# HGRN2 levels: one fill of two PSUM banks, joint factor tiles, both pairs' projections first, a general PSUM ring of two

## The chip, the cores and the metric

The kernel runs on one core of a Trainium2 chip. The metric is the device time of one execution in microseconds. A core has TensorE (PE, with the weight loads shown apart as PEld), VectorE (DVE), ScalarE (ACT), GpSimd (POOL) and SyncE (SP, which issues DMAs here). Each engine executes its own instructions in order; engines wait for each other by semaphores.

## The reference, cut to what matters

The program is one step of a two-layer backbone on 128 prompt and 256 sample tokens (384 together, width 1024). Layer 0 has two mixers behind one input projection: windowed attention with 8 heads of 64 (A), and a bidirectional HGRN2 with 4 heads of 128 (B), a gated linear recurrence:

```python
qa, ka, va, qb, ib, ff, fb, gb = split(h @ w_in)
f = lb + (1 - lb) * sigmoid(z);   k = 1 - f            # a gate for each direction
# one direction, over time t (qc = q * dk**-0.5, cum = cumsum(log f))
attn[t, s] = sum_k qc[t, k] * exp(cum[t, k] - cum[s, k]) * k[s, k]     # s <= t
o = attn @ v  +  (qc * exp(cum)) @ s_start             # within a chunk + from the state
s_end = exp(last) * s_start + (k * exp(last - cum))^T @ v
ob = rms_norm(o_fwd + o_bwd, gnorm) * silu(gb)
y = concat([oa, ob]) @ w_out
```

Then come a residual with layer norm, a gated feed-forward network, and layer 1 with two other attention mixers, which the change leaves alone. All is in fp32.

## The kernel before, in words

Every large product is made of three fp32r matmuls (lines 127 to 129): the weights are split into a high part wh (ACT, line 122) and a low part wl (DVE, line 123) as they arrive, the activations into hH and hL. Weights go through rings of three tiles.

The kernel is written in a framework with a scheduler: it sets each engine's order beforehand, from the order in which the program is written, shifted by an offset for each part of it (the table AHEAD; a larger number comes earlier), and from which operands it expects to be ready. Tiles come from pools; a tile whose slots are all in use must wait until one is read out.

PSUM in layer 0 is opened as three slots "ps" of one bank (attention's scores s, transposed probabilities pt, values ov, and in hg_out tk, up, ho, ty), three "pj" for projections and output accumulators o, one "lv" for the levels, and one more for the adaLN vectors of later stages (ada_acc, line 203; such a step is four matmuls).

mixer_ab (line 818) computes layer 0's mixers. HGRN2's four heads go as two pairs. For a pair, proj_fm makes q and two gates, with features on partitions (2 heads x 384 tokens in a row of 768). hg_levels (line 861) then builds the matrix attn for each of six blocks of 128 tokens (2 heads x 3). It does that by doubling: a diagonal step, then seven levels with spans of 1, 2, 4 to 64 tokens. The factors Fq and Fk (forward), Bq and Bk (backward) hold q and k times the gates' products up to the span's border. In a level ACT copies halves of the four factors into a mixed key tile Kc and query tile Qc (lines 890 to 893), PE multiplies six blocks (line 872, tile hs), DVE merges the part of the result that belongs to the level into the matrix AT with a mask (copy_predicated, line 911), and DVE multiplies the factors by the next gates' products (line 900), and those among themselves (nB, lines 907 and 908). The six blocks need two fills of the one "lv" bank, four blocks and two.

hg_out (line 921) follows for a pair: keys transposed (tk, 933), the states' update (up, 938), the output (ho, 950 to 954), its sum of squares (ACT, 958), an inverse root on POOL (line 110), scaling and gate on DVE (963, 968), a transposition (ty, 971), and the split into hH and hL (132, 133).

attention (line 725) runs through pairs of tiles: two scores s (722, with the mask at 1116) for a query tile, row maximum (640), bias nm (608), exponential (643), transposes pt (673), their evacuation by ACT or DVE (656, 658), ov (679), and the put of the result as hH and hL (663, 664). out_first starts the output projection on what is there (tiles o). The boundary then completes it; its dense stretch begins where no more of hg_out is awaited.

The order of the program at the end of mixer_ab is: a_ctx, the projections of keys and values and of queries, the levels of pair 0, the projections of pair 1, those of the values ib and the gate gb, the levels of pair 1, attention, hg_out 0, out_first, hg_out 1.

Of the kernel before, what the change touches and what calls it, by code (L numbers as in the profile page):

```python
# [20 lines left out]
P = 128  # L21
D = 1024
KD = 8
NTOK = 384
# [5 lines left out]
AHEAD = {"w": 1500, "w0": -700, "lv0": -30, "lv1": 0, "attA": 400, "attC": 400, "attD": 100, "fin": 500, "qs": -1500,  # L30
# [11 lines left out]
def tile_backbone_step(ctx, tc, I, O):  # L42
# [10 lines left out]
    psum = {}  # L53
# [7 lines left out]
    def lvt(name):  # L61
        return psum["lv"].tile([P, 512], F32, tag="lv", name=name)
# [755 lines left out]
    def mixer_ab():  # L818
# [4 lines left out]
        M = Slots(es, {"one": (1, 0), "pr": (4, 768), "pt": (6, 512), "qS": (2, 1536), "qf": (3, 768),  # L823
                       "X": (8, 768), "at": (2, 768), "vB": (2, 768), "kq": (3, 768), "t2": (5, 512),
# [4 lines left out]
        def hg_tiles():  # L829
            return M.tile("qf", F32), [M.tile("X", F32) for _ in range(4)], [M.tile("qf", F32) for _ in range(2)]  # L830
# [9 lines left out]
        def ev_f(pr, d, X, f):  # L840
            def ev(j, acc):
                c = slice(4 * d + 2 * pr + j, 4 * d + 2 * pr + j + 1)
                sl = slice(j * NTOK, (j + 1) * NTOK)
                sg = M.sm.tile([P, NTOK], F32, tag="sg", name="sg")
                nc.scalar.activation(sg, acc, AF.Sigmoid)
                nc.vector.tensor_scalar(out=X[2 + d][:, sl], in0=sg, scalar1=C["nomlb"][:, c],
                                        scalar2=C["omlb"][:, c], op0=ALU.mult, op1=ALU.add)
                nc.vector.tensor_scalar(out=f[d][:, sl], in0=sg, scalar1=C["omlb"][:, c], scalar2=C["lb"][:, c],
                                        op0=ALU.mult, op1=ALU.add)
                nc.vector.tensor_scalar(out=f[d][:, sl], in0=f[d][:, sl], scalar1=1e-30, scalar2=None, op0=ALU.max)  # L850
            return ev

        def hg_proj(pr):
            q, X, f = hg_tiles()
            proj_fm(w, 768 + 256 * pr, ev_q(q))
            proj_fm(w, 1792 + 256 * pr, ev_f(pr, 0, X, f))
            proj_fm(w, 2304 + 256 * pr, ev_f(pr, 1, X, f))
            return q, X, f


        def hg_levels(q, X, f, out):
            Fq, Bq, Fk, Bk = X
            nc.vector.tensor_tensor(out=Fq, in0=q, in1=f[0], op=ALU.mult)
            nc.vector.tensor_tensor(out=Bq, in0=q, in1=f[1], op=ALU.mult)
            AT = M.tile("at", F32).rearrange("p (b t) -> p b t", b=6)

            def scores(Kc, Qc, take):
                for b0, nb in ((0, 4), (4, 2)):
                    pp = lvt("hs").rearrange("p (b t) -> p b t", b=4)
                    for b in range(nb):  # L870
                        bs = slice((b0 + b) * P, (b0 + b + 1) * P)
# [3 lines left out]
            def diag(pp, bl, nb):  # L875
                nc.vector.tensor_tensor(out=AT[:, bl, :], in0=pp, in1=ident.unsqueeze(1).to_broadcast([P, nb, P]),
                                        op=ALU.mult)

            Kc = M.tile("kq", F32)
            nc.vector.tensor_tensor(out=Kc, in0=Fk, in1=Bk, op=ALU.add)  # L880
            scores(Kc, q, diag)
            yield
            Bf, Bb = f
            for lv in range(7):
                m = 1 << lv
                G = 2 * NTOK // (2 * m)
                V = lambda a: a.rearrange("p (g h m) -> p g h m", h=2, m=m)
                Kc = M.tile("kq", F32)
                Qc = M.tile("kq", F32)
# [5 lines left out]
                bf = Bf.rearrange("p (g h w) -> p g h w", h=2, w=w_)[:, :, :, 0]  # L895
                bb = Bb.rearrange("p (g h w) -> p g h w", h=2, w=w_)[:, :, :, 0]
                bc = lambda a: a.unsqueeze(2).to_broadcast([P, G, m])
                for eng, T, hh, fac in ((nc.vector, Fk, 0, bf[:, :, 1]), (nc.vector, Bk, 1, bb[:, :, 0]),
                                        (nc.vector, Fq, 1, bf[:, :, 0]), (nc.vector, Bq, 0, bb[:, :, 1])):
                    eng.tensor_tensor(out=V(T)[:, :, hh, :], in0=V(T)[:, :, hh, :], in1=bc(fac), op=ALU.mult)  # L900
                if lv == 0:
                    nB = M.sm.tile([P, 2, NTOK], F32, tag="nB", bufs=1, name="nB")
                    Bf, Bb = nB[:, 0, :], nB[:, 1, :]
                    nf, nb_ = Bf, Bb
                else:
                    nf, nb_ = bf[:, :, 0], bb[:, :, 0]
# [3 lines left out]
                def merge(pp, bl, nb):  # L910
                    nc.vector.copy_predicated(AT[:, bl, :],
                                              C["lmask"][:, lv, :].unsqueeze(1).to_broadcast([P, nb, P]), pp)
# [4 lines left out]
            for d, B in enumerate((Bf, Bb)):  # L917
                nc.vector.tensor_copy(out=eb[:, d, :], in_=B.rearrange("p (g w) -> p g w", w=64)[:, :, 0])
            out.extend((AT, eb))

        def hg_out(pr, X, AT, eb, vB):
            Fq, Bq, Fk, Bk = X
# [85 lines left out]
        st0 = hg_tiles()  # L1008
# [71 lines left out]
        ps1 = open_psum(3, 3, 1)  # L1080
# [70 lines left out]
        with ahead("lv1"):  # L1151
            drain(hg_levels(*st1, lv1))
# [301 lines left out]
    for l in range(2):  # L1454
# [6 lines left out]
        with tc.tile_pool(name="bnd", bufs=1) as b1:  # L1461
# [3 lines left out]
                     x_in if l == 0 else x_mid, False, first, lvt if l == 0 else None, part)  # L1465
# [63 lines left out]
```

## Time and profile before

| | us |
|---|---|
| three runs | 1095.95, 1096.12, 1098.69; median 1096.12 |
| the profiled execution | 1095.94 |
| its span, first instruction to last | 1094.1 |
| input projections of layer 0 | 58.7 to 188.3 |
| attention, levels, hg_out 0 | 188.3 to 235.0 |
| levels 2 to 6 of pair 1, hg_out 1 | 235.0 to 272.1 |
| dense output projection of layer 0 | from 272.1 |

Times inside the execution count from the start of the span. A busy share is the part of a stretch in which an engine executes; a wait is the idle time before an instruction, with the engine and instruction that ended it. The granted clock is a share of TensorE's full speed. A line of the timeline groups records of one operation that follow each other ("x4" is four of them); a matmul of fp32 operands of 128x128 is two records, a transposition one. PE's matmuls are pipelined, so that one that takes 0.39 us can be followed by another after 0.22.

### The profile page before, as it was taken

Reading aid. Unit: us, or ns where it says so; the run is one execution under the profiler, and the core shown is the slowest. Engines: PE = TensorE matmul, PEld = TensorE weight load, DVE = VectorE, ACT = ScalarE, POOL = GpSimd, SP = SyncE. Lnnn points to the kernel's source line nnn. Section 1 sums busy time; section 2 is a strip of 40 time slices with the busy share of each in tenths; the row PEclk is TensorE's granted clock in tenths of the full one; section 3 lists DMA queues with packets and bytes.
Section 4 is the critical chain, followed back from the end, with each engine's and each line's share of the span. In section 5 each row is a group of like instructions: output and inputs, shape, how many; then the busy total and the mean of one; then the engine's idle time right before and its main releaser. Section 6 shows DMA issues by size and latency. Waiting matters only on the chain. (4 is left out here: it accounts for less than half of the span.)

```text
span 1094.1 us, 15881 instructions
## 1 busy us (share of the span) xinstructions
PE 1036.0 (95%) x6105; PEld 870.7 (80%) x6105; DVE 660.6 (60%) x1140; ACT 440.8 (40%) x804; POOL 120.0 (11%) x166
## 2 busy tenths in 40 slices
PE   5999999987999999999999998979899999999996
PEld 4788767555889999897778786666589999998885
DVE  2575855686598458458236875765489464443237
ACT  2365645363253323232223547545254333332231
POOL 0021201101110000000000343213130000000004
PEclk8999999997999999999999999989999999999998
DMA  9874243484047776766655431144126555543431
GB/s 305 258 222 124 86 142 123 140 275 164 23 150 219 249 221 219 232 210 214 237 190 159 152 108 45 35 150 165 47 79 194 151 172 153 159 135 116 135 116 58
DMA packets 114354, 173.13 MB, mean 158 GB/s; under 512 B 9419, under 2 KB 82150, under 8 KB 114278
## 3 DMA queue, kind: packets, MB, share of 16 engines
q1 hardware_dynamic: 113526, 171.78, 50.0%
q8 instruction: 48, 0.79, 0.3%
q10 hardware_dynamic: 752, 0.34, 0.1%
q14 instruction: 28, 0.23, 0.1%
HBM read 167.84 MB, written 4.24 MB: 157 GB/s over the span
## 5 line engine op out<-in xcount | busy, mean ns | idle before, releaser
L123 DVE TENSOR_TENSOR wl<-wr,wh 128x1024 fp32r<-128x1024 f32 (+4 forms) x200 | 235.7, 1182 | 234.9 <-ACT wh L122 232.3
L122 ACT ACTIVATE wh<-wr 128x1024 fp32r<-128x1024 f32 (+4 forms) x200 | 202.4, 1015 | 347.3 <-PE pf L128 124.0
L127 PE MATMUL pf<-hH,wh 128*128 128x384 f32 x688 | 232.7, 338 | 0.0
L129 PE MATMUL pf<-hH,wl 128*128 128x384 f32 x688 | 232.7, 338 | 0.0
L128 PE MATMUL pf<-hL,wh 128*128 128x384 f32 x688 | 232.6, 338 | 0.0
L129 PEld LDWEIGHTS pf<-hH,wl 128*128 128x128 f32 x688 | 129.4, 188 | 3.1 <-issue 3.1
L128 PEld LDWEIGHTS pf<-hL,wh 128*128 128x128 f32 x688 | 129.4, 188 | 2.7 <-issue 2.6
L127 PEld LDWEIGHTS pf<-hH,wh 128*128 128x128 f32 x688 | 129.4, 188 | 2.3 <-issue 2.2
L128 PE MATMUL o<-wl,aH 128*128 128x512 f32 (+1 forms) x280 | 101.2, 361 | 0.7 <-DVE wl L123 0.7
L127 PE MATMUL o<-wh,aH 128*128 128x512 f32 (+1 forms) x280 | 101.3, 362 | 0.4 <-DVE a L1175 0.4
L129 PE MATMUL o<-wh,aL 128*128 128x512 f32 (+1 forms) x280 | 101.0, 361 | 0.0
L129 PE MATMUL pj<-wh,hL 128*128 128x512 f32 (+3 forms) x240 | 89.0, 371 | 2.0 <-POOL hL L344 1.8
L127 PE MATMUL pj<-wh,hH 128*128 128x512 f32 (+3 forms) x240 | 89.2, 377 | 0.3 <-ACT vA L1106 0.2
L261 DVE SCALAR_TENSOR_TENSOR part<-ar,cT,part 128x512 f32<-128x512 f32 x112 | 80.2, 744 | 15.3 <-DMA ar<-in_w_ada 15.2
L128 PE MATMUL pj<-wl,hH 128*128 128x512 f32 (+3 forms) x240 | 89.0, 371 | 0.0
L110 POOL TENSOR_TENSOR ve<-ve,nhalf 128x1 f32<-128x1 f32 x12 | 7.0, 583 | 617.7 <-DVE ve L530 336.1
L127 PEld LDWEIGHTS o<-wh,aH 128*128 128x128 f32 x280 | 52.9, 189 | 10.2 <-issue 1.4
L128 PEld LDWEIGHTS o<-wl,aH 128*128 128x128 f32 x280 | 52.9, 189 | 9.0 <-DVE wl L123 1.0
L129 PEld LDWEIGHTS o<-wh,aL 128*128 128x128 f32 x280 | 52.8, 188 | 9.2 <-issue 1.2
L129 PEld LDWEIGHTS pj<-wh,hL 128*128 128x128 f32 x240 | 45.1, 188 | 12.2 <-POOL hL L344 2.7
L127 PEld LDWEIGHTS pj<-wh,hH 128*128 128x128 f32 x240 | 44.8, 188 | 10.4 <-issue 2.7
L128 PEld LDWEIGHTS pj<-wl,hH 128*128 128x128 f32 x240 | 45.1, 188 | 8.6 <-issue 1.4
(318 smaller groups left out, 1542.7 us busy)
## 6 DMA issues: line engine op xcount, KB each, us to landing
ar<-in_w_ada SPq DMA_DIRECT2D x80, 512.0 KB
wr<-in_w_ffn_down SPq DMA_DIRECT2D x44, 512.0 KB
wr<-in_w_ffn_gate SPq DMA_DIRECT2D x40, 512.0 KB
wr<-in_w_ffn_up SPq DMA_DIRECT2D x40, 512.0 KB
wr<-in_w_in_ab SPq DMA_DIRECT2D x18, 512.0 KB
ar<-in_w_ada SPq DMA_DIRECT2D x32, 256.0 KB
wr<-in_w_out SPq DMA_DIRECT2D x16, 512.0 KB
wr<-in_w_in_ab SPq DMA_DIRECT2D x16, 256.0 KB
```

The costliest lines, as they stand in the source:

```text
L110: nc.gpsimd.tensor_tensor(out=out, in0=v, in1=nhalf[:, :n], op=ALU.pow)
L122: nc.scalar.activation(hi, raw, AF.Copy)
L123: nc.vector.tensor_tensor(out=lo, in0=raw, in1=hi.bitcast(F32), op=ALU.subtract)
L127: nc.tensor.matmul(out, lh, rh, start=start, stop=False)
L128: nc.tensor.matmul(out, lh, rl, start=False, stop=False)
L129: nc.tensor.matmul(out, ll, rh, start=False, stop=stop)
L261: nc.vector.scalar_tensor_tensor(out=dst, in0=raw[:, j], scalar=sc, in1=dst, op0=ALU.mult, op1=ALU.add)
```

## The change

A level's six blocks fill one "lv" tile of two banks at once; diagonal and merge are one DVE operation of 768 elements each instead of two of 512 and 256. The "ps" ring pays for the bank with one of its three slots. Forward and backward key factors lie in one tile, query factors in another (backward first), so that strided views take both halves: ACT copies a level's Kc and Qc with two operations instead of four, DVE multiplies K in one operation instead of two (Q stays two, on halves), and nB is one operation instead of two. Fq is formed after the diagonal fill. In the program, the projections of pair 1 and both pairs' levels now stand ahead of the projections of keys, values, queries and gate, and the levels' offsets go up. Over the program DVE has 48 fewer rows of order, ACT 32 fewer, and 12 table loads instead of 16.

```diff
-AHEAD = {"w": 1500, "w0": -700, "lv0": -30, "lv1": 0, ...
+AHEAD = {"w": 1500, "w0": -700, "lv0": 1000, "lv1": 800, ...
     def lvt(name):
-        return psum["lv"].tile([P, 512], F32, tag="lv", name=name)
+        return psum["lv"].tile([P, 2, 512], F32, tag="lv", name=name)
-        M = Slots(es, {..., "qf": (3, 768), "X": (8, 768), ...
+        M = Slots(es, {..., "f": (1, 1536), "X": (4, 1664), ...
+        def mixed(X, m):
+            v = X[:, 0:2 * (N2 + m)].rearrange("p (h r) -> p h r", h=2)[:, :, 0:N2]
+            return v.rearrange("p h (g a i) -> p h g a i", a=2, i=m)[:, :, :, 0, :]
             def scores(Kc, Qc, take):
-                for b0, nb in ((0, 4), (4, 2)):
-                    pp = lvt("hs").rearrange("p (b t) -> p b t", b=4)
-                    for b in range(nb):
-                        nc.tensor.matmul(pp[:, b, :], Kc[:, bs], Qc[:, bs], start=True, stop=True)
-                    take(pp[:, 0:nb, :], slice(b0, b0 + nb), nb)
+                pp = lvt("hs").rearrange("p a (b t) -> p (a b) t", b=4)
+                for b in range(6):
+                    nc.tensor.matmul(pp[:, b, :], Kc(b), Qc(b), start=True, stop=True)
+                take(pp[:, 0:6, :])
...
-                nc.scalar.activation(V(Qc)[:, :, 1, :], V(Fq)[:, :, 1, :], AF.Copy)
-                nc.scalar.activation(V(Qc)[:, :, 0, :], V(Bq)[:, :, 0, :], AF.Copy)
-                nc.scalar.activation(V(Kc)[:, :, 0, :], V(Fk)[:, :, 0, :], AF.Copy)
-                nc.scalar.activation(V(Kc)[:, :, 1, :], V(Bk)[:, :, 1, :], AF.Copy)
+                for c, x in ((Kc, Km), (Qc, Qm)):
+                    nc.scalar.activation(c.rearrange("p (g h i) -> p g h i", h=2, i=m),
+                                         x.rearrange("p h g i -> p g h i"), AF.Copy)
+                scores(blk(Kc), blk(Qc), merge)
...
-                for eng, T, hh, fac in ((nc.vector, Fk, 0, bf[:, :, 1]), (nc.vector, Bk, 1, bb[:, :, 0]),
-                                        (nc.vector, Fq, 1, bf[:, :, 0]), (nc.vector, Bq, 0, bb[:, :, 1])):
-                    eng.tensor_tensor(out=V(T)[:, :, hh, :], in0=V(T)[:, :, hh, :], in1=bc(fac), op=ALU.mult)
+                nc.vector.tensor_tensor(out=Km, in0=Km, in1=bc(kf), op=ALU.mult)
+                nc.vector.tensor_tensor(out=Qm[:, 1], in0=Qm[:, 1], in1=bc(bv[:, 0, :, 0]), op=ALU.mult)
+                nc.vector.tensor_tensor(out=Qm[:, 0], in0=Qm[:, 0], in1=bc(bv[:, 1, :, 1]), op=ALU.mult)
...
-                nc.vector.tensor_tensor(out=nf, in0=bf[:, :, 0], in1=bf[:, :, 1], op=ALU.mult)
-                nc.vector.tensor_tensor(out=nb_, in0=bb[:, :, 0], in1=bb[:, :, 1], op=ALU.mult)
-                scores(Kc, Qc, merge)
+                nc.vector.tensor_tensor(out=nB, in0=bv[:, :, :, 0], in1=bv[:, :, :, 1], op=ALU.mult)
...
-        ps1 = open_psum(3, 3, 1)
+        ps1 = open_psum(2, 3, 1)
...
         lv0, lv1 = [], []
+        st1 = hg_proj(1)
+        with ahead("lv0"):
+            drain(hg_levels(*st0, lv0))
+        with ahead("lv1"):
+            drain(hg_levels(*st1, lv1))
         a_ctx()
         proj_tm(w, 512, 256, evac_kv)
         proj_tm(w, 0, 512, evac_q)
-        with ahead("lv0"):
-            drain(hg_levels(*st0, lv0))
-        st1 = hg_proj(1)
         with ahead("ib"):
             proj_tm(w, 1280, 512, ev_v)
         with ahead("gb"):
             proj_tm(w, 2816, 512, ev_g)
-        with ahead("lv1"):
-            drain(hg_levels(*st1, lv1))
```

The order shows what moves. Three places follow. First PE where the last levels of pair 1 stand. Before, they lie behind the projections, between attention (pt, ov), adaLN steps (ada_acc) and hg_out 0 (tk, up):

```order
L129 MATMUL o_2430<-wh,hL 128x512
L673 MATMUL pt<-ident,pr 128x128 x4
L872 MATMUL hs<-kq 128x128 x2
L203 MATMUL ada_acc<-ar,cT 32x256 x5
L679 MATMUL ov<-pt,vA 64x256
L203 MATMUL ada_acc<-ar,cT 32x256 x3
L679 MATMUL ov<-pt,vA 64x256 x3
L933 MATMUL tk<-ident,X 128x128 x4
L679 MATMUL ov<-pt,vA 64x256 x2
L872 MATMUL hs<-kq 128x128 x4
L203 MATMUL ada_acc<-ar,cT 32x256 x4
```

Now the last fill of all (hs, six blocks) stands among the gate's projections (pj):

```order
L882 MATMUL hs<-kq 128x128 x6
L127 MATMUL pj_1808<-wh,hH 128x512
L128 MATMUL pj_1808<-wl,hH 128x512
L129 MATMUL pj_1808<-wh,hL 128x512
L128 MATMUL pj_1801<-wl,hH 128x512
L129 MATMUL pj_1801<-wh,hL 128x512
L127 MATMUL pj_1801<-wh,hH 128x512
L709 MATMUL pt<-ident,pr 128x128 x8
```

So the levels of pair 1 left the part of the program that follows the projections.

Second PE in attention, between two scores s of one query tile. Before, level matmuls hs lie around them, beside output products o:

```order
L722 MATMUL s<-kT,qS 128x384
L1116 MATMUL s<-bmaskR,identR 128x128
L129 MATMUL o_2429<-wh,hL 128x512
L129 MATMUL o_2430<-wh,hL 128x512
L872 MATMUL hs<-kq 128x128 x2
L722 MATMUL s<-kT,qS 128x384
L1116 MATMUL s<-bmaskR,identR 128x128
L673 MATMUL pt<-ident,pr 128x128 x4
L203 MATMUL ada_acc<-ar,cT 32x256 x4
L872 MATMUL hs<-qf,kq 128x128 x4
```

Now:

```order
L722 MATMUL s<-kT,qS 128x384
L1122 MATMUL s<-bmaskR,identR 128x128
L203 MATMUL ada_acc<-ar,cT 32x256 x4
L127 MATMUL o_2331<-wh,hH 128x512
L128 MATMUL o_2331<-wl,hH 128x512
L127 MATMUL o_2332<-wh,hH 128x512
L128 MATMUL o_2332<-wl,hH 128x512
L722 MATMUL s<-kT,qS 128x384
L1122 MATMUL s<-bmaskR,identR 128x128
L129 MATMUL o_2331<-wh,hL 128x512
L129 MATMUL o_2332<-wh,hL 128x512
```

Between the scores stand only adaLN steps and output products; the levels' matmuls are gone.

Third ACT at the end of the projections, where the gate's sigmoid (line 1133, now 1139, on pj) needs another table of functions than the exponential (line 643). Before, the three sigmoids stand together:

```order
L1133 ACT_TABLE_LOAD
L1133 ACTIVATE t_1812<-pj_1719 128x512
L1133 ACTIVATE t_1817<-pj_1726 128x512
L1133 ACTIVATE t_1822<-pj_1733 128x512
L643 ACT_TABLE_LOAD
L643 ACTIVATE pr,sm<-s,nm 128x384 x2
L623 ACTIVATE es<-es 128x4
L658 ACTIVATE pt<-pt 128x512
```

Now:

```order
L1139 ACT_TABLE_LOAD
L1139 ACTIVATE t_1887<-pj_1794 128x512
L643 ACT_TABLE_LOAD
L643 ACTIVATE pr,sm<-s,nm 128x384 x2
L1139 ACT_TABLE_LOAD
L1139 ACTIVATE t_1892<-pj_1801 128x512
L1139 ACTIVATE t_1897<-pj_1808 128x512
L643 ACT_TABLE_LOAD
L643 ACTIVATE pr,sm<-s,nm 128x384 x2
```

The first two exponentials moved between the sigmoids, which makes four table loads of two.

## Rows read from the trace of the kernel before

**Rows 1.** The page: busy us of each engine, share of the span, instructions.

```profile
PE 1036.0 (95%) x6105; PEld 870.7 (80%) x6105; DVE 660.6 (60%) x1140; ACT 440.8 (40%) x804; POOL 120.0 (11%) x166
```

**Rows 2.** Busy time by stretch: us, engines' busy (instructions), PE clock, DMA share, GB/s.

```profile
58.70:188.30 129.60, 128.68 (x713) 98.00 (x713) 85.25 (x167) 71.91 (x139) 20.45 (x22) 1.00 0.46 137
188.30:235.00 46.70, 46.16 (x335) 30.12 (x334) 30.87 (x68) 22.64 (x56) 8.03 (x12) 1.00 0.57 180
235.00:272.10 37.10, 25.43 (x143) 19.19 (x142) 26.79 (x73) 17.19 (x44) 3.08 (x5) 0.80 0.59 196
```

**Rows 3.** Waits of PE, 235.0 to 272.1 us: us in total, times, longest.

```profile
PE hs L872 <- ACT kq L893: 2.6, 3, 1.4
...
PE hs L872 <- DVE at L911: 1.5, 2, 0.8
```

**Rows 4.** Busy time by shorter stretches, columns as in group 2.

```profile
235.00:247.00 12.00, 6.68 (x52) 4.46 (x50) 10.87 (x29) 7.69 (x18) 0.20 (x1) 1.00 0.75 246
247.00:257.50 10.50, 8.00 (x30) 6.73 (x31) 8.17 (x24) 3.17 (x8) 0.69 (x1) 0.51 0.16 50
...
267.50:278.00 10.50, 9.08 (x21) 6.21 (x21) 5.11 (x11) 0.25 (x2) 0.70 (x1) 0.51 0.33 101
```

**Rows 5.** PE's timeline, 256 to 273 us: start, us, engine, line, operation, records.

```profile
256.19 1.06 PE L933 MATMUL tk<-ident,X 128*128 128x128 f32 x4
...
257.67 0.39 PE L128 MATMUL o<-wl,hH 128*128 128x512 f32 x1
257.90 0.39 PE L129 MATMUL o<-wh,hL 128*128 128x512 f32 x1
...
262.65 0.39 PE L953 MATMUL ho<-t,X 128*128 128x128 f32 x2
262.87 0.39 PE L954 MATMUL ho<-t,X 128*128 128x128 f32 x2
...
272.11 0.77 PE L127 MATMUL o<-wh,hH 128*128 128x512 f32 x1
```

**Rows 6.** Timeline of PE, ACT, DVE in attention, 205 to 208 us.

```profile
205.11 0.91 PE L722 MATMUL s<-kT,qS 64*128 64x384 f32 x2
...
206.11 0.62 PE L673 MATMUL pt<-ident,pr 128*128 128x128 f32 x4
...
206.34 0.55 DVE L640 TENSOR_REDUCE mx<-s 128x1 f32<-128x384 f32 x1
...
206.67 0.64 PE L203 MATMUL ada_acc<-ar,cT 128*32 128x256 f32 x8
...
207.75 0.15 DVE L608 SCALAR_TENSOR_TENSOR nm<-mx,nsink 128x2 f32<-128x2 f32 x1
...
207.93 0.58 ACT L643 ACTIVATE pr<-s,nm 128x384 f32<-128x384 f32 x1 [0.27 <-DVE nm L608]
```

**Rows 7.** DVE by line and shape, 58.7 to 272.1 us: busy us, mean ns, idle.

```profile
L123 DVE TENSOR_TENSOR wl<-wr,wh 128x1024 fp32r<-128x1024 f32 x28 | 34.8, 1252 | 14.2 <-ACT wh L122 14.2
L900 DVE TENSOR_TENSOR X<-X,nB 128x384 f32<-128x384 f32 x48 | 26.2, 576 | 1.0 <-ACT kq L892 0.8
L911 DVE COPY_PREDICATED at<-lmask,hs 128x512 f32<-128x512 uint8 x14 | 10.2, 731 | 4.4 <-PE hs L872 4.2
...
L911 DVE COPY_PREDICATED at<-lmask,hs 128x256 f32<-128x256 uint8 x14 | 6.2, 442 | 9.2 <-PE hs L872 9.2
L656 DVE COPY pt<-pt 128x512 f32<-128x512 f32 x7 | 4.8, 688 | 5.0 <-PE pt L673 5.0
...
L880 DVE TENSOR_TENSOR kq<-X 128x768 f32<-128x768 f32 x2 | 1.9, 946 | 0.0
...
L664 DVE TENSOR_TENSOR hL<-ov,hH 128x256 fp32r<-128x256 f32 x4 | 1.7, 420 | 2.0 <-ACT hH L663 2.0
```

**Rows 8.** ACT's timeline at the end of the projections.

```profile
187.80 1.28 ACT L643 ACT_TABLE_LOAD   x1
189.09 0.58 ACT L643 ACTIVATE pr<-s,nm 128x384 f32<-128x384 f32 x1
```

More of the change, by code (lines that the diff above doesn't have):

```diff
@@ L822, in mixer_ab, with half, hg_tiles @@
         es = ExitStack()
-        M = Slots(es, {"one": (1, 0), "pr": (4, 768), "pt": (6, 512), "qS": (2, 1536), "qf": (3, 768),
-                       "X": (8, 768), "at": (2, 768), "vB": (2, 768), "kq": (3, 768), "t2": (5, 512),
+        M = Slots(es, {"one": (1, 0), "pr": (4, 768), "pt": (6, 512), "qS": (2, 1536), "f": (1, 1536),
+                       "X": (4, 1664), "at": (2, 768), "vB": (2, 768), "kq": (3, 768), "t2": (5, 512),
                        "gB": (1, 1536)})
         gB = M.tile("gB", F32).rearrange("p (a t j v) -> p a t j v", a=2, t=3, j=2)
-        def hg_tiles():
-            return M.tile("qf", F32), [M.tile("X", F32) for _ in range(4)], [M.tile("qf", F32) for _ in range(2)]
+        N2 = 2 * NTOK
+        def half(X, i):
+            return X[:, i * N2:(i + 1) * N2]
+        def mixed(X, m):
+            v = X[:, 0:2 * (N2 + m)].rearrange("p (h r) -> p h r", h=2)[:, :, 0:N2]
+            return v.rearrange("p h (g a i) -> p h g a i", a=2, i=m)[:, :, :, 0, :]
+        def hg_tiles(f):
+            X = [M.tile("X", F32) for _ in range(2)]
+            return half(X[1], 1), X, M.tile(f, F32)
         def ev_q(q):
@@ L879, in hg_levels @@
             Kc = M.tile("kq", F32)
             nc.vector.tensor_tensor(out=Kc, in0=Fk, in1=Bk, op=ALU.add)
-            scores(Kc, q, diag)
+            blk = lambda a: (lambda b: a[:, b * P:(b + 1) * P])
+            scores(blk(Kc), blk(q), diag)
+            nc.vector.tensor_tensor(out=Fq, in0=q, in1=half(f, 0), op=ALU.mult)
             yield
-            Bf, Bb = f
+            B, W = f, N2
             for lv in range(7):
                 m = 1 << lv
[L886 to L889, printed above, removed]
-                nc.scalar.activation(V(Qc)[:, :, 1, :], V(Fq)[:, :, 1, :], AF.Copy)
-                nc.scalar.activation(V(Qc)[:, :, 0, :], V(Bq)[:, :, 0, :], AF.Copy)
-                nc.scalar.activation(V(Kc)[:, :, 0, :], V(Fk)[:, :, 0, :], AF.Copy)
-                nc.scalar.activation(V(Kc)[:, :, 1, :], V(Bk)[:, :, 1, :], AF.Copy)
-                w_ = max(1, m // 2)
-                bf = Bf.rearrange("p (g h w) -> p g h w", h=2, w=w_)[:, :, :, 0]
-                bb = Bb.rearrange("p (g h w) -> p g h w", h=2, w=w_)[:, :, :, 0]
-                bc = lambda a: a.unsqueeze(2).to_broadcast([P, G, m])
-                for eng, T, hh, fac in ((nc.vector, Fk, 0, bf[:, :, 1]), (nc.vector, Bk, 1, bb[:, :, 0]),
-                                        (nc.vector, Fq, 1, bf[:, :, 0]), (nc.vector, Bq, 0, bb[:, :, 1])):
-                    eng.tensor_tensor(out=V(T)[:, :, hh, :], in0=V(T)[:, :, hh, :], in1=bc(fac), op=ALU.mult)
@@ new lines, in hg_levels, with merge @@
+                G = N2 // (2 * m)
+                Km, Qm = mixed(K, m), mixed(Q, m)
+                def merge(pp):
+                    nc.vector.copy_predicated(AT, C["lmask"][:, lv, :].unsqueeze(1).to_broadcast([P, 6, P]), pp)
+                Kc, Qc = [M.tile("kq", F32) for _ in range(2)]
+                for c, x in ((Kc, Km), (Qc, Qm)):
+                    nc.scalar.activation(c.rearrange("p (g h i) -> p g h i", h=2, i=m),
+                                         x.rearrange("p h g i -> p g h i"), AF.Copy)
@@ L910, in merge @@
-                def merge(pp, bl, nb):
-                    nc.vector.copy_predicated(AT[:, bl, :],
-                                              C["lmask"][:, lv, :].unsqueeze(1).to_broadcast([P, nb, P]), pp)
-                scores(Kc, Qc, merge)
+                    B, W = M.sm.tile([P, N2], F32, tag="nB", bufs=1, name="nB"), NTOK
+                    nB = B.rearrange("p (d g) -> p d g", d=2)
+                else:
+                    nB = bv[:, :, :, 0]
+                nc.vector.tensor_tensor(out=nB, in0=bv[:, :, :, 0], in1=bv[:, :, :, 1], op=ALU.mult)
@@ L915, in hg_levels @@
                 yield
             eb = M.sm.tile([P, 2, 6], F32, tag="eb", name="eb")
-            for d, B in enumerate((Bf, Bb)):
-                nc.vector.tensor_copy(out=eb[:, d, :], in_=B.rearrange("p (g w) -> p g w", w=64)[:, :, 0])
+            nc.vector.tensor_copy(out=eb, in_=B.rearrange("p (d g w) -> p d g w", d=2, w=64)[:, :, :, 0])
             out.extend((AT, eb))
         def hg_out(pr, X, AT, eb, vB):
-            Fq, Bq, Fk, Bk = X
+            Fk, Bk, Bq, Fq = half(X[0], 0), half(X[0], 1), half(X[1], 0), half(X[1], 1)
@@ L1464, in tile_backbone_step @@
             boundary(b1, x_t, l, 0, lambda k: hH[:, k, :], lambda k: hL[:, k, :], ORDER[l], I["w_out"][l], lambda: ms,
-                     x_in if l == 0 else x_mid, False, first, lvt if l == 0 else None, part)
+                     x_in if l == 0 else x_mid, False, first, (lambda name: lvt(name)[:, 0, :]) if l == 0 else None, part)
             with tc.tile_pool(name="part", bufs=1) as pp, tc.tile_pool(name="ffn", bufs=1) as fp:
```

31 lines of the change are left out of this document (14 added, 17 removed).

## The prediction

> **What bounds the kernel now.** The busy line comes first [rows 1]: TensorE (PE) works 95 of 100 parts of the span, so a gain has to come from the few places where it doesn't. The table by stretches [rows 2] shows where they are in layer 0. From 58.7 to 188.3 us, the input projections, PE is busy 128.7 of 129.6 us, and from 188.3 to 235.0, attention and adaLN steps, 46.2 of 46.7: the reader is to see that nothing can be gained in either by moving work of other engines. From 235.0 to 272.1 it is busy 25.4 of 37.1 us. There stand levels 2 to 6 of the second head pair and that pair's hg_out, and the table of waits [rows 3] says what PE stood for: copies of the level factors on ScalarE (ACT), products on VectorE (DVE). This is a chain over three engines with nothing to put in its holes. The granted clock is 1.00 in the first two stretches and 0.80 in the third; at 247.0 to 257.5 and 267.5 to 278.0 it is 0.51, the lower of its two levels, 1.2 GHz [rows 4]. Before the first fall PE had been waiting for half of its time. The second reaches into the dense output projection that begins at 272.1. So about 12 us of waits and some 3 to 4 us of slow clock lie between 235 and 278 us, and that is all that the change can reach.
>
> **The change, part by part.** Every level moves in among the projections. In the order of before, 37 of the 96 level matmuls stand ahead of the last projection; in the new order all 96 do, with the second pair's last fill some 18 rows ahead of it. In exchange 6 score tiles, 16 transposes of probabilities, 6 value products and 5 adaLN matmuls move behind it. The sum goes stage by stage, each with its end on the clock of the trace.
>
> *Projections.* A 128x128 matmul takes 0.22 us from start to start (262.65 to 262.87, [rows 5]), so 59 level matmuls add 13.0 us. A score tile with its mask takes 1.0 us (205.11 to 206.11, [rows 6]), four transposes 0.62 with one run-out in it, so 0.11 to 0.16 each, 0.11 taken, a value product like a level matmul 0.22, and four adaLN matmuls 0.64 [rows 6]: 5.8 + 1.8 + 1.3 + 0.8 = 9.7 us leave. PE's packed work grows by 3.3 us. DVE must now feed sixteen fills there. From [rows 7], a level costs a K product of 768 elements at the price of L880, 0.95, two Q products of 384, 1.15, and one merge of 768: the two merges of 512 and 256 differ by 0.29, so 768 costs 1.02, where two of them cost 1.17 before. That is 3.12 x 14 = 43.7 us, with some 5 for the running products and 7.6 for the diagonal fills 56; 31 of it is in this stretch already. DVE's 85.3 us [rows 2] become 106 to 111, beside 133 us of PE. That hides, with one part in six to spare, since fills wait in PSUM while PE has projections; I take 0.5 us of stalls. ACT's four copies of a level become two over as many elements, on an engine that is busy 71.9 of 129.6 us [rows 2], and cost nothing on the path while that holds. Projections end at 188.3 + 3.3 + 0.5 = 192.1 us.
>
> *Attention behind them.* What is left is ten score tiles, four sets of 12 transposes and 6 value products. Where before took its holes away with level matmuls, the new order has only 16 adaLN steps of 0.64 us [rows 6] and 30 output-projection matmuls of 0.23 (257.67 to 257.90, [rows 5]), 17.1 us. At the same time the general PSUM ring drops from three slots to two, and two score tiles fill it. A query tile then runs: score 1.0, score 1.0, reduce 0.55, bias 0.15, the two exponentials with their sums 1.2, and with the waits between engines 4.3 us [rows 6], since the next score waits until its slot is read. The second half of a pair runs: transposes 0.62, evacuation 0.69, transposes 0.62, evacuation 0.69, value products 1.3, put on ACT and DVE 0.42 each [rows 6, 7], about 5.0. Five query tiles and four halves in a row are 21.5 + 20.0 = 41.5 us, of which PE works 9.7 + 5.4 + 5.2 = 20.3; the other 21.2 are holes for the 17.1 of filler. PE's packed work alone is 37.4 us. So it takes 37.4 to 41.5 if all filler fits, and up to 58.6 if none does. Walking the new order row by row, with the filler where it stands, I get 43; three weight loads of ACT (wh) and of DVE (wl, 1.25 each [rows 7]) stand ahead of the last put on these engines and hold it by 2 more. I take 45, so attention ends at 237.1.
>
> *The two hg_outs.* Before, the first pair's hg_out was spread among attention. Now both stand behind it, the second pair's first transpose behind the first pair's last. One alone took from 256.19 to 272.1 us, 15.9 [rows 5]. Its chain runs over PE, ACT, POOL and DVE, and its holes can't be filled by the 18 output matmuls left. Two cost 31.8: 268.9 us. The last transposes' halves must still be put before the dense output projection reads them, between 0 and 1.2 us; I take 0.7. The dense stretch begins at 269.6, against 272.1: **-2.5 us**.
>
> *After that.* The orders are the same from some 50 rows into the dense stretch on. The ring of two delays the boundary's first tile by some 0.8 us; the dense stretch of before lost up to 2.9 us at half clock (272.1 to 278 at 0.51, [rows 4]) which may or may not be lost again. I set these against each other, with -2.9 and +0.8 as ends. The pools in SBUF (two wide factor tiles for four, one for three) move no transfer, since weights go through rings that the change doesn't touch; SP's queue gets the same loads.
>
> *Tables.* The new order has four loads of ACT's tables around the end of the projections, as the gate's sigmoid alternates with the first exponentials; before it had two. A load takes 1.28 us and the exponential follows at 189.09, right at its end [rows 8]. Two more loads, 2.6 us, lie under the last projections. The Trainium skill ("ScalarE: Activation LUTs", What ACT_TABLE_LOAD costs) counts a drain of 1.38 us beside each load of 1.28, 2.66 us in all. By that the four would hold the first exponentials 3.3 us longer and the time would be 1096.7; the trace shows 0.01 us between load and exponential, so the sum goes without it.
>
> The profiled execution took 1095.94 us with a span of 1094.1, 0.2 us under the median of 1096.12. 1095.94 - 2.5 = **1093.4 us**. A difference under 0.3%, 3.3 us, can't be told from no change.
>
> **The rivals.** *More is gained.* The clock stays at its upper level through tail and dense stretch, as it does while PE is packed [rows 2], and filler fits the holes: attention costs 41 rather than 45, the dense stretch gives back 2.9 less 0.8. -2.5 - 4 - 2.1 = -8.6, 1087.3 us. For it: PE busy 46.2 of 46.7 in the attention of before. Against it: that was on three slots, with levels as filler, and hg_out as a serial chain stays.
>
> *The ring of two serialises attention: slower.* A score tile can't be issued ahead, and PE being in order, filler behind a blocked score is blocked too. The price is the part of the 17.1 us that no longer fits. It decides from 5.8 us on (the 2.5 gained and 3.3). With half of it outside, 8.6 less the 1.5 already counted (43 for 41.5), the time is 1100.5 us; with all of it 1109. For it: the second score of a tile stands right behind adaLN steps in the new order, and a put waits behind weight loads. Against it: four adaLN matmuls stand between most pairs of scores, ahead of the wait.
>
> *The clock falls within attention.* On two slots PE has short holes at every tile, and one stretch of 10.5 us at 0.51 with 9.1 busy [rows 4] costs some 5 us against the upper level: 1098.4. Against it: before fell only where PE was busy about half, 6.7 of 12 us [rows 4]. The Trainium skill ("TensorE: Matmul & The Clock Gate", A second HAM failure mode: psum-queue depth-cycling) tells of a kernel whose PE idled briefly at each change of PSUM bank and whose clock swung between its levels for it. In the trace the attention stretch on three slots shows 1.00 [rows 2], which speaks against it as far as three slots do.
>
> *DVE bounds the projections.* Early fills cost 5 to 6.5 us of DVE each, where PE has 5 to 6 of projections between them. If the merges then run late, the chain Q product, copy, fill stalls PE's order: some +6 on the forecast, 1099.4. Against it: 106 to 111 of 133.
>
> That the change doesn't do what it says, levels ahead of the projections' end, the new order excludes: the fills stand there and PE executes in order.
>
> **How the numbers follow.** Forecast 46 in 100, own range -6 to +2; more gained 24; serial attention 16; clock 7; DVE 7. Of the forecast 18 are faster by over 0.3%, 27 within, 1 slower. Of more gained 22 and 2 within; serial 1 within, 15 slower; clock 4 and 3; DVE 3 and 4. That makes faster 0.40, same 0.37, slower 0.23. The range is 1085 to 1103: the lower end is the second case with 2 us for a quicker hg_out, left out below it about 6 in 100; the upper lets in serial attention with two thirds of the filler lost and leaves out some 12.
>
> **What would show it.** Right: all level matmuls start before about 190 us; projections end at 191 to 193; DVE busy above 80 of 100 up to there; PE waits no longer for level copies or merges, but in attention for exponentials and puts (scores and transposes), some 4 us in all; two hg_outs of about 16 us in a row; the dense stretch begins near 270. Wrong: projections ending past 195 (DVE); attention of more than 50 us with scores waiting for slots, or a clock under 0.9 there; a dense stretch that begins near 262, which would mean that hg_out was never a chain of 16 us but was stretched by levels and slow clock.

## The result: slower by half a per cent

The changed kernel takes 1102.91 us (median of 12 runs), the kernel before, run beside it, 1096.58: ratio 1.0055, 95% interval 1.0039 to 1.0071, that is +6.0 us, +4.3 to +7.8. The forecast was -2.5. In the profiled executions (1103.58 and 1095.94 us) the dense stretch of the output projection begins at 278.6 us instead of 272.1; what follows adds little.

By stages, with the columns of [rows 2]: the projections, attention, hg_out 0 and hg_out 1 of the changed kernel.

```profile
58.70:186.70 128.00, 126.30 (x771) 105.32 (x770) 101.87 (x174) 71.06 (x123) 11.84 (x16) 1.00 0.43 133
186.70:237.20 50.50, 43.69 (x289) 21.74 (x288) 17.06 (x42) 15.26 (x38) 9.77 (x17) 0.93 0.56 173
237.20:259.20 22.00, 13.91 (x73) 11.12 (x71) 11.49 (x24) 10.31 (x25) 2.10 (x3) 0.84 0.69 238
259.20:278.60 19.40, 12.31 (x64) 9.52 (x64) 10.58 (x25) 8.82 (x24) 2.08 (x3) 0.83 0.40 123
```

The projections are as full as before (126.3 of 128.0 us) although all level matmuls are in them, DVE is busy 101.9 us there, and they end at 186.7. Of the 92 us from there to the dense stretch PE is busy 70: attention takes 50.5 us at a clock of 0.93 (before, [rows 2] show 46.2 busy of 46.7 at 1.00 there), and the hg_outs, one after the other, 22.0 and 19.4 us at 0.84 and 0.83, where [rows 5] had one in 15.9. The waits of PE in attention, with the columns of [rows 3]:

```profile
PE ada_acc L203 <- DMA ar<-in_w_ada: 4.4, 5, 1.6
PE pt L673 <- ACT pr L643: 1.8, 2, 1.0
```

and in the hg_outs:

```profile
PE ty L977 <- DVE kq L969: 4.2, 2, 3.2
PE up L944 <- ACT t L941: 3.1, 3, 2.2
PE o L127 <- ACT hH L663: 2.9, 1, 2.9
PE o L127 <- ACT hH L132: 1.6, 2, 1.2
```

The level copies and merges of [rows 3] are gone from these lists. In their place stand adaLN weights that come late, and in the hg_outs waits for ACT and DVE. What these two did is in their timeline:

```profile
237.48 2.95 ACT L122 ACTIVATE wh<-wr 128x1024 fp32r<-128x1024 f32 x3 [1.83 <-PE ov L679]
...
240.33 0.36 ACT L663 ACTIVATE hH<-ov 128x256 fp32r<-128x256 f32 x1
...
240.75 0.52 PE L127 MATMUL o<-wh,hH 128*128 128x512 f32 x1 [2.86 <-ACT hH L663]
...
247.61 0.28 ACT L964 ACTIVATE jk<-ho 128x128 f32<-128x128 f32 x1
...
250.61 1.06 ACT L122 ACTIVATE wh<-wr 128x1024 fp32r<-128x1024 f32 x1 [2.64 <-DMA wr<-in_w_out]
...
251.58 0.26 ACT L964 ACTIVATE jk<-ho 128x128 f32<-128x128 f32 x1
251.70 1.22 DVE L123 TENSOR_TENSOR wl<-wr,wh 128x1024 fp32r<-128x1024 f32 x1 [1.61 <-ACT wh L122]
...
254.49 0.48 PE L977 MATMUL ty<-ident,kq 128*128 128x128 f32 x2 [3.20 <-DVE kq L969]
```

At 237.48 ACT starts three weight splits (wh), and the put of attention's last values (hH L663) and the copy of the transposed keys stand behind them in its order; an output matmul of PE waits 2.86 us for that put. At 250.61 ACT has been idle for 2.64 us before a split whose weights had not come, while squares (L964) of products that PE had finished at 249.5 stood behind it; the transposition ty starts 3.20 us late. This repeats in hg_out 1 (1.95 us of idle before a split at 262.43, there of weights of the feed-forward network).

### The profile page after: what moved, and what is told of

It is laid out like the page before. It is cut to its first block, busy times and chain, and to the rows that moved or that the text cites. A ratio compares the mean times of both kernels' runs of the same rounds, so it can differ in the third digit from the quotient of the medians.

```text
span 1101.8 us, 15808 instructions
## 1 busy us (share of the span) xinstructions
PE 1032.8 (94%) x6105; PEld 871.7 (79%) x6105; DVE 656.6 (60%) x1094; ACT 433.9 (39%) x772; POOL 113.8 (10%) x166
## 4 chain that ended last, share of the span: by engine, by line
PE 72%; DMA 11%; DVE 8%; ACT 3%; issue 3%; POOL 2%; SPq 1%; ACTq 0%; DVEq 0%; POOLq 0%
PE pf L129 9%; PE pf L127 9%; PE pf L128 9%; PE o L127 7%; PE o L128 7%; PE o L129 7%; DMA ar<-in_w_ada 6%; PE pj L129 4%; PE pj L127 4%; PE pj L128 4%; PE ada_acc L203 3%; DVE wl L123 2%; PE hs L882 2%; PE s L722 2%; DVE part L261 2%
## 5 line engine op out<-in xcount | busy, mean ns | idle before, releaser
L129 PEld LDWEIGHTS pj<-wh,hL 128*128 128x128 f32 x240 | 45.1, 188 | 11.3 <-POOL hL L344 2.8
```

Source lines behind the costliest of these rows:

```text
L129: nc.tensor.matmul(out, ll, rh, start=False, stop=stop)
```

## The experiments

Each ratio is to the kernel before, run beside it on the same chip, with its 95% interval.

**Two slots without the rest.**

```diff
 # the kernel before
-        ps1 = open_psum(3, 3, 1)
+        ps1 = open_psum(2, 3, 1)
```

> The kernel before with one edit: the general PSUM ring has two slots instead of three; levels, tiles and program order stay. Theory A (the changed kernel is slow because the two hg_outs stand in a row behind attention and weight splits waiting for DMA stand inside their chain): the ring costs 0 to 2 us here, ratio 1.000 to 1.002. Theory B (the ring of two serialises scores and transposes): +4 to +8 us, ratio 1.004 to 1.007, with score tiles and transposes waiting for exponentials and evacuations in 188 to 235 us.

Measured: 1.0134 (1.0109 to 1.0159), 1109.18 us. More than either theory gave: theory A's claim that the ring is nearly free falls, and B's price was too low. Nor are B's waits there: up to hg_out 0 scores and transposes wait 1.2 us in all. The stretches, attention with levels, hg_out 0, hg_out 1:

```profile
185.50:243.50 58.00, 53.17 (x377) 33.72 (x377) 42.09 (x106) 28.28 (x68) 12.86 (x16) 0.97 0.45 141
243.50:265.10 21.60, 15.69 (x89) 13.18 (x88) 14.31 (x33) 10.77 (x26) 2.10 (x3) 0.84 0.71 238
265.10:284.20 19.10, 12.09 (x67) 9.53 (x65) 9.93 (x24) 8.77 (x23) 2.09 (x3) 0.84 0.40 126
```

Attention takes 58 us. In the kernel before it takes 33.7, counted from the projections' end to its last value product (ov); the row, and three of PE's timeline, hg_out 0's first and last transposition among them:

```profile
188.30:222.00 33.70, 33.57 (x226) 20.25 (x225) 20.71 (x48) 13.99 (x34) 6.80 (x10) 1.00 0.46 134
```

```profile
220.74 0.65 PE L933 MATMUL tk<-ident,X 128*128 128x128 f32 x4
221.32 0.65 PE L679 MATMUL ov<-pt,vA 128*64 128x256 f32 x4
...
255.76 0.64 PE L971 MATMUL ty<-ident,kq 128*128 128x128 f32 x2
```

So hg_out 0 did not run inside attention before either: it began about 1 us ahead of attention's end and went on to 256 beside the last levels of pair 1. What the third slot shortens is attention. With two slots the scheduler's order leaves 8 of its score tiles behind the projections (16 records of line 722), with three it leaves 4. The two hg_outs then look like those of the changed kernel.

**The rest without the two slots.**

```diff
 # the changed kernel
-                pp = lvt("hs").rearrange("p a (b t) -> p (a b) t", b=4)
-                for b in range(6):
-                    nc.tensor.matmul(pp[:, b, :], Kc(b), Qc(b), start=True, stop=True)
-                take(pp[:, 0:6, :])
+                for b0, nb in ((0, 4), (4, 2)):
+                    pp = lvt("hs").rearrange("p (b t) -> p b t", b=4)
+                    for b in range(nb):
+                        nc.tensor.matmul(pp[:, b, :], Kc(b0 + b), Qc(b0 + b), start=True, stop=True)
+                    take(pp[:, 0:nb, :], slice(b0, b0 + nb), nb)
...
-        ps1 = open_psum(2, 3, 1)
+        ps1 = open_psum(3, 3, 1)
```

> The changed kernel with the PSUM part undone: fills of four and two blocks into one bank, ring of three; joint factor tiles, offsets and program order stay. The scheduler then lets the last levels of pair 1 slip behind the projections again, into attention and hg_out. Theory A: the levels fill holes of the tail as before, hg_out 0 is spread among attention, so the time is near the kernel before, 0.998 to 1.002, although the order of the program is the new one. Theory B: near the kernel before too, but then before_ring2 must be slow. Theory C (the order of the program and the offsets cost the time): 1.004 to 1.007.

Measured: 0.9912 (0.9893 to 0.9932), 1084.5 us. Better than any theory said. The trade of a slot for a wider fill thus costs 1.0055 - 0.9912 = 0.0143, some 16 us, and the rest of the change gains 10.

```profile
192.30:227.50 35.20, 35.09 (x238) 20.99 (x236) 24.29 (x52) 18.29 (x36) 10.28 (x12) 1.00 0.39 124
227.50:248.20 20.70, 18.67 (x142) 12.94 (x141) 14.30 (x37) 10.24 (x25) 2.27 (x3) 1.00 0.85 276
248.20:264.60 16.40, 11.40 (x66) 8.48 (x65) 10.79 (x24) 9.26 (x24) 2.92 (x3) 0.81 0.85 290
```

From the projections' end to hg_out 0 it takes 35.2 us with PE busy 35.1, and 6 score tiles stand behind the projections, where the changed kernel has 10. hg_out 0 begins 2 us before attention's last value products (229.5) and takes 20.7 us beside the last levels, which end at 241; it is not inside attention here either. Against the changed kernel attention is shorter by 15.3 us, the hg_outs by 1.3 and 3.0, and the projections end 5.6 later: 14.0 us to the dense stretch. So the larger part of the loss lies in attention. How much of it is the tiles that moved behind the projections, and how much the two slots within attention, is not shown.

**Output weights left out, in both kernels.**

```diff
             def load(i, *a):
                 k = order[i]
-                hi, lo = wload(w[k * P:(k + 1) * P, :], 1, D, *a)
+                if first and first[1] is None:
+                    hi, lo = [x.rearrange("p a b -> p (a b)").unsqueeze(1) for x in C["tw"]]
+                else:
+                    hi, lo = wload(w[k * P:(k + 1) * P, :], 1, D, *a)
...
```

> The changed kernel; left out are five of the six later loads of the output projection's weights in layer 0 (one of the out_second loads is used for all), with their splits on ACT and DVE; the matmuls stay. Theory A: the hg_outs lose the splits that wait for DMA, 237.2 to 278.6 us becomes 32 to 34 us, and the dense stretch begins at 269 to 271: -7 to -9 us against the changed kernel, ratio to the kernel before 0.997 to 0.999. Theory B: attention keeps its length and the hg_outs theirs within 2 us, ratio 1.003 to 1.006.

> The kernel before with the same loads left out, as the measure of what they cost there. Theory A: two splits each on ACT and DVE stand in the chain of hg_out 1, some 2 to 3 us, and nothing else waits for them, so -2 to -4 us, ratio 0.996 to 0.998, much less than the same loads are worth in the changed kernel. Theory B has no reason for a difference between the two kernels: the same gain in both.

Measured: 0.9991 (0.9976 to 1.0006) and 0.9943 (0.9921 to 0.9965): -7 us against the changed kernel, -6 against the one before. In the changed kernel the hg_outs became as short as expected:

```profile
191.60:248.00 56.40, 46.87 (x289) 24.61 (x288) 19.20 (x44) 17.15 (x40) 10.73 (x17) 0.85 0.54 173
248.00:263.10 15.10, 11.03 (x73) 8.74 (x71) 7.12 (x21) 7.37 (x22) 2.17 (x3) 1.00 0.70 243
263.10:278.00 14.90, 10.23 (x67) 8.27 (x68) 7.06 (x22) 5.21 (x19) 2.18 (x3) 1.00 0.07 20
```

They take 15.1 and 14.9 us at a clock of 1.00, 11.4 us less than in the changed kernel; two splits are left in the first and none in the second. So the splits and their late weights do stretch hg_out. The dense stretch still began only 1.3 us earlier, at 277.3 and not at 269 to 271: in this execution the projections ended 4.9 us later, with a clock of 0.74 from 58.7 to 72.0 (1.00 in that of the changed kernel), and attention took 56.4 us, 5.9 more; why, stays open. From the projections' end to the dense stretch it is 85.7 us for 91.9. In the kernel before, the dense stretch began 1.9 us earlier without the loads (270.2) and ran at 1.00 from its start, where [rows 4] show 0.51. So the same loads cost nearly as much there, and they don't explain the difference of the two kernels, as theory A had it.

**adaLN's weights left out.**

```diff
             for k in range(KD):
-                raw = adap.tile([P, 2, 512], F32, tag="ar", name="ar")
-                dma(out=raw, in_=I["w_ada"]...)
+                if k == 0:
+                    raw = adap.tile([P, 2, 512], F32, tag="ar", name="ar")
+                    dma(out=raw, in_=I["w_ada"]...)
```

> The changed kernel; left out are seven of the eight weight loads of each later adaLN vector of layer 0 (the eight steps use one load), the matmuls stay. Theory F (attention on the ring of two lasts 50 us because adaLN steps wait for their DMA, and the clock falls in these waits): attention 40 to 43 us, dense stretch near 270, -7 to -9 us against the changed kernel, ratio to the kernel before 0.997 to 0.999. If the DMA only fills holes that are there anyway: attention 47 us or more, ratio 1.002 to 1.006.

Measured: 1.0081 (1.0054 to 1.0108), no gain at all. Theory F falls. The waits for DMA were in the shadow of others, which now show:

```profile
191.00:243.20 52.20, 45.78 (x282) 24.92 (x281) 16.14 (x44) 14.29 (x38) 9.60 (x16) 0.87 0.09 26
```

and the waits of PE in that stretch:

```profile
PE pt L674 <- ACT pr L644: 3.4, 2, 1.7
PE s L723 <- ACT pr L644: 2.2, 2, 1.1
```

Attention takes 52.2 us with DMA at 0.09 of its time. PE now waits for exponentials, at the transposes and at the scores: a score's slot is read out by the exponential, so the wait at s, 2.2 us, is the ring.

**The order alone, and the tiles alone**, on the ring of three with fills of four and two. The edit for the order alone:

```diff
 # the kernel before
+        st1 = hg_proj(1)
+        with ahead("lv0"):
+            drain(hg_levels(*st0, lv0))
+        with ahead("lv1"):
+            drain(hg_levels(*st1, lv1))
         a_ctx()
...
```

> The kernel before with the program order and the offsets of the changed one (pair 1's projections and both pairs' levels first), but separate factor tiles, four copies and fills of four and two in one bank, ring of three. Pair 1's q and gates take slots of the values' and queries' tiles. If the gain of 11 us of after_ring3 is the order's: 0.989 to 0.993. If it comes from the joint tiles, which take work off DVE and ACT: 0.998 to 1.002.

> The program order, the offsets, the ring of three and the fills of four and two of the kernel before, with the joint factor tiles: two copies on ACT instead of four in a level, three products on DVE instead of four, one nB instead of two. The order alone gave 0.9974 and both together 0.9912. If the tiles give the rest by themselves: 0.991 to 0.995 (the chain of a level gets shorter by about 1 us, and some 8 levels stand bare between 188 and 255 us). If they help only with the levels early: 0.997 to 1.001.

Measured: 0.9974 (0.9955 to 0.9993) and 0.9990 (0.9977 to 1.0003). Neither gives the 0.9912 of both together; the tiles help only with the levels early, and the order is worth more than 3 us only with the joint tiles. Why, stays open.

**The old order on the ring of two.**

```diff
 # the changed kernel
-AHEAD = {... "lv0": 1000, "lv1": 800, ...
+AHEAD = {... "lv0": -30, "lv1": 0, ...
...
-        st1 = hg_proj(1)
...
         proj_tm(w, 0, 512, evac_q)
+        with ahead("lv0"):
+            drain(hg_levels(*st0, lv0))
+        st1 = hg_proj(1)
...
```

> The changed kernel with the program order and offsets of the kernel before; joint tiles, fills of two banks and ring of two stay. The levels of pair 1 stand behind the projections again. If the order hurts on a ring of two because it takes the levels out of the tail's holes: ratio 0.997 to 1.001, faster than the changed kernel. If the order helps on two slots as on three (0.9974): 1.006 to 1.010, slower than the changed kernel.

Measured: 1.0000 (0.9981 to 1.0019): on two slots the new order costs 6 us, on three it gains. From the projections' end to hg_out 0, then the two hg_outs:

```profile
180.50:231.80 51.30, 49.25 (x355) 28.84 (x353) 32.39 (x70) 21.33 (x45) 10.41 (x16) 0.97 0.54 170
231.80:252.80 21.00, 12.04 (x71) 9.78 (x70) 11.21 (x24) 9.71 (x24) 2.10 (x3) 0.92 0.70 251
252.80:272.20 19.40, 12.17 (x65) 9.60 (x65) 8.96 (x22) 8.28 (x22) 2.19 (x3) 0.83 0.34 104
```

The projections end 6 us earlier, since levels are left out of them, and attention, now with levels until 208 us in it, takes 51.3 us: as long as the 50.5 without them. On two slots the 37 level matmuls behind the projections cost little there (8 score tiles stand beside them, not 10); moved into the packed projections they take most of their full price, 6 us of the 8 that 37 make at 0.22.

**hg_out in banks of its own.**

```diff
 # the changed kernel; in the second kernel hg_out's PE work is also held behind attention
-                tp = pst("tk").rearrange("p (i d) -> p i d", i=4)
+                hg2 = lvt("hg").rearrange("p a (i d) -> p a i d", i=4)
+                tp = hg2[:, 0]
...
-                up = pst("up").rearrange("p (i d) -> p i d", i=4)
+                up = hg2[:, 1]
...
-                op = pst("ho").rearrange("p (j d) -> p j d", j=4)
+                op = hg3[:, t // 2, 2 * (t % 2):2 * (t % 2) + 2]
...
-AHEAD = {... "ho0": -100, "ho1": -30, ...
+AHEAD = {... "ho0": 600, "ho1": 600, ...
```

> The changed kernel, with the ring of two and the fill of two banks kept, but hg_out's transposes, state updates and outputs (tk, up, ho) go into the two level banks, free by then, instead of the general ring, and both hg_outs get an offset of 600. The scheduler then puts hg_out 0 among attention, its first step right behind the projections. Theory D (the ring costs time because hg_out must take its slots behind attention's, so the two run one after the other): the dense stretch begins at 250 to 258 instead of 279, ratio to the kernel before 0.985 to 0.992. Theory E (the ring of two slows attention by itself): attention still takes 50 us or more and ends at 237 or later, hg_out 1 still follows it, ratio 0.995 to 1.002.

> after_hg_own_banks with one edit: hg_out's instructions on TensorE are held behind the last value product of attention, so that the two hg_outs follow attention as in the changed kernel, while they keep banks of their own. Theory D (what costs is the place of hg_out, which a ring shared with attention forces): the whole gain is lost again, ratio to the kernel before 1.003 to 1.008, the two hg_outs take 35 to 41 us behind attention. If banks of their own were worth the time by themselves: 0.989 to 0.994.

Measured: 0.9890 (0.9855 to 0.9925), 1084.09 us, and 1.0215 (1.0189 to 1.0241). The first came out as theory D had it, dense stretch at 254.4 included. In it, attention with both hg_outs in it:

```profile
188.80:246.20 57.40, 54.45 (x384) 31.92 (x383) 24.45 (x71) 22.85 (x67) 13.33 (x22) 1.00 0.53 166
246.20:254.50 8.30, 5.63 (x34) 3.99 (x32) 6.50 (x13) 5.16 (x12) 0.70 (x1) 1.00 0.85 305
```

Attention isn't faster, 57.4 us, but PE is busy 54.5 of them at a clock of 1.00, and 8.3 us later the dense stretch is reached. So hg_outs inside attention, in banks of their own, are 18 us ahead of the changed kernel, which has them behind it. That doesn't make the lost slot a lost overlap: the kernel before and after_ring3 didn't have them there. The two edits, banks and offsets, came together; the offsets alone, on the ring of two, were not run. In the second kernel the hg_outs take some 57 us behind attention, not 35 to 41: they share one tile, and PE waits 11.9 us in them for the scaling on DVE. It shows that banks of their own gain nothing by themselves, and as it is slower than the changed kernel it doesn't show what the place alone is worth.

**Attention's transposes and values in the level banks.**

```diff
 # the changed kernel, pair_2 and prompt_2
-            tp = pst("pt").rearrange("p (b q) -> p b q", b=2)
+            if g == 0:
+                two = A.two("pt2")
+            tp = two[:, g % 2].rearrange("p (b q) -> p b q", b=2)
...
-        ov = A.bank("ov")[:, 0:256]
+        ov = two[:, 1, 0:256]
...
```

> The changed kernel with attention's transposes and value products (pt, ov) in the two level banks; the scores and hg_out keep the ring of two. Theory D: hg_out still stands behind all scores in the ring, so only part is won; attention, whose transposes no longer wait for a slot, ends some 5 to 8 us earlier, ratio 0.997 to 1.001. Theory E (the ring of two in attention itself is the larger part of the loss): attention at 35 to 38 us as on three slots, 12 us or more won, ratio 0.991 to 0.995.

Measured: 0.9969 (0.9948 to 0.9990), 1091.5 us, 9 us better than the changed kernel, just outside D's range and short of E's; its interval reaches into both. From the projections' end to hg_out 0, then the two hg_outs:

```profile
186.10:225.80 39.70, 35.94 (x229) 19.06 (x229) 13.26 (x35) 13.39 (x37) 7.38 (x13) 0.91 0.46 146
225.80:244.50 18.70, 16.92 (x143) 12.17 (x141) 8.86 (x28) 7.20 (x23) 4.35 (x7) 1.00 0.59 191
244.50:268.00 23.50, 15.46 (x78) 12.35 (x76) 14.70 (x27) 13.45 (x27) 2.13 (x3) 0.81 0.79 276
```

hg_out 0 begins after 39.7 us instead of 50.5 and overlaps with the end of attention, so the two are compared together: 58.4 us instead of 72.5. hg_out 1 stands alone for 23.5 us at 0.81. Which made the 9 us, the shorter attention or this overlap, is not shown.

**hg_out written between attention's steps, on three slots.**

```diff
 # after_ring3; hg_out is a generator of 16 steps for both pairs
+            for _ in attention(M, Att(...)):
+                for _ in range(3):
+                    next(hgs, None)
...
```

> after_ring3 (joint tiles, new order, ring of three, fills of four and two) with hg_out as steps that are written between the steps of attention, three to one, so that the ring's slots alternate between both. Theory D: hg_out 0 and 1 run beside attention and the last pair's hg_out no longer stands alone; dense stretch at 250 to 258, ratio 0.980 to 0.987. If the tail is held by the DMA of adaLN and output weights instead, no more than after_ring3: 0.989 to 0.993.

Measured: 1.0156 (1.0121 to 1.0191). A miss. The ring's slots go in program order, so scores now wait for hg_out's slots:

```profile
PE s L722 <- ACT pr L643: 3.0, 2, 1.5
...
PE s L722 <- DVE kq L973: 1.2, 1, 1.2
```

The second half of the stretch behind the projections:

```profile
225.60:279.20 53.60, 46.68 (x209) 29.21 (x210) 19.78 (x56) 17.68 (x57) 8.90 (x15) 0.75 0.02 5
```

The scheduler put every score of the sample tiles behind the projections, and the clock was 0.75 there.

## Why the prediction was wrong, point by point

*Levels out of the tail.* Right as a mechanism: all 16 fills run before 182 us, and level waits are gone. The prices on DVE were right (a merge of 768 elements took 1.034 us for 1.02, a K product 0.954 for 0.95), its total there was 101.9 us for 106 to 111, and DVE bounded nothing.

*Projections.* Forecast end 192.1, measured 186.7: 5.4 us too late, in the change's favour. The level matmuls entered at their price (busy 24.2 us for 11.8 before, 12.4 more for the 13.0), but what left took more than its price: PE's busy time fell by 4.0 us for adaLN steps (0.8 in the sum), 6.9 for scores (5.8), 2.7 for transposes (1.8) and 1.7 for value products (1.3). Part of it is also luck of the execution: in after_no_wout, after_no_ada_dma and own_banks_behind the projections, with the same levels in them, ended at 191.7, 191.1 and 189.2, with a clock of 0.74, 0.87 and 0.87 from 58.7 to 72.0, where the changed kernel's execution had 1.00.

*Attention.* Forecast 45, measured 50.5: the step that said that filler fits the holes. The size of the loss is near the rival's (the ring of two serialises attention), and after_no_ada_dma and after_old_order show a length of 51 to 52 us that neither adaLN's DMA nor level matmuls change. By an estimate some 3 us of it are clock: from 209.0 to 218.0 it was 0.62.

```profile
209.00:218.00 9.00, 7.42 (x49) 3.46 (x41) 1.63 (x4) 1.26 (x5) 2.26 (x4) 0.62 0.56 171
```

The rows show a clock below 1.00 in attention in the kernels on two slots with PE waiting (0.93, 0.87 in after_no_ada_dma, 0.97 in after_old_order), and 1.00 where PE stayed busy, on three slots (after_ring3) and on two (after_hg_own_banks). With waits it was 0.75 on three slots too (ring3_mixed). So the rival built on the Trainium skill ("TensorE: Matmul & The Clock Gate", A second HAM failure mode: psum-queue depth-cycling) came true in part: the trace agrees that short idle times of PE and a falling clock go together; that cycling through PSUM banks is behind it, no run here shows, and two slots alone don't do it.

*The hg_outs.* Forecast 31.8, measured 41.4. This is the step that failed most: it took 15.9 us from a chain with two splits in it (at a clock of 0.82), and priced two chains with nine splits in and ahead of them at the same. after_no_wout, on the same two slots, has them at 15.1 and 14.9 us with two splits, so what made 41.4 of 30 is the late splits, with the lower clock that came along, and not the ring. That the hg_outs would stand one after the other was read rightly from the order. That hg_out 0 was spread among attention before, as the prediction says, is wrong: it ran from 220.7 to 256, all but the first microsecond behind attention, beside the levels of pair 1 (the rows stand with the first experiment).

*The sum.* -5.4 + 5.5 + 9.6 - 0.7 (the last puts, in the 19.4 already) = +9.0 us, from 269.6 forecast to 278.6. Against the kernel before, with attention counted to its last value product: the projections end 1.6 us earlier, attention takes 50.6 us for 33.7, and the time from there to the dense stretch is 41.3 for 50.1, which makes -1.6 + 16.9 - 8.8 = +6.5. The forecast had +3.8, +11.3 and -17.6: the gain in the tail was half of what was expected. The lower clock came back at the dense stretch, for 3.5 us at 0.51 where before had 5.7 at 0.50. The measured time lies inside the stated range, by 0.1 us, but by luck: the upper end stood for a loss in attention alone, and no rival gave the hg_outs a higher price.

*Tables.* The exponential followed its load at once again (184.60 + 1.28, then 185.90), so the drain that the Trainium skill ("ScalarE: Activation LUTs", What ACT_TABLE_LOAD costs) counts beside a load isn't seen here either.

What the prediction lacked is the question what a stage takes in its new company. It knew that ten score tiles and both hg_outs would stand behind the projections without the levels. It priced the first as if all filler would fit and the second by a chain with fewer splits.

## What to carry to other kernels

A ring's slots are handed out in the order of the program, and the scheduler sets the order by them. So taking a slot changes what stands where: here 8 score tiles were left behind the projections instead of 4 (the first experiment) and 10 instead of 6 (the second), and the trade of a slot for a wider fill cost some 16 us although hardly a wait on the ring is seen. Matmuls that fill holes cost little there; moved into a packed stretch they cost most of their time unless the holes close. Before a chain's length is used as a price, look at what stood in its engines' orders, weight splits above all, and at what ran beside it. A later stage that gets banks of its own and a place inside the earlier one can win more than the slot: of the kernels here after_hg_own_banks (0.9890) and after_ring3 (0.9912) beat both that were compared.

## What the runs showed of the hardware

When PE had waits of one to three us in it, the granted clock of the stretch was mostly lower: 0.81 to 0.84, once 0.92, over hg_outs that stood alone with late splits in them, 1.00 over the same two with only two splits left (after_no_wout). So a late split of 1 to 3 us may have been paid twice, in the wait and in the clock, which the sum had not foreseen. Of the runs none separates the two.
